# Attention bias tables: one copy of each row in DRAM, read with a stride of one number between partitions and with reversed keys

## The chip, the cores and the metric

The kernel runs on one core of one Trainium2 chip. The metric is the device time of one execution in microseconds (us). The engines are TensorE (PE, matrix products), VectorE (DVE), ScalarE (ACT), GpSimd (POOL) and SyncE (SP), which here only issues transfers.

## What is computed

The reference chains two networks on 256 tokens of width 1024, in float32. The first is one layer: a gated feed-forward network (`ffn1`), attention, a second feed-forward network (`ffn2`) and a per-layer embedding. The second is two layers with a latent attention, a long convolution and a feed-forward network, with modulation vectors (`w_mod`). The change touches only the attention of the first layer. It has 16 heads in two mixers, both with a causal window and an additive bias that depends on the head and on the distance of query and key alone:

```python
rel = jnp.arange(bq)[:, None] + max_dist - jnp.arange(nk)[None, :]
bias = rel_bias[t5_bucket(rel * stride)].astype(jnp.float32)
...
logits = jnp.where(valid[None, :, None, None], logits + bias, NEG_INF)
```

## The kernel before

Every product of two float32 matrices is made of three products of split operands (a rounded part and a rest, `hi` and `lo`): `gemm` (L126 to L128) and `gemm_T` (L139 to L141). Weights come in tiles `raw` of 512 KB, two k tiles each, which SP loads (L111, in `units`). ACT rounds each k tile to `whi` (L115) and DVE takes the rest, `wlo` (L116). There are 4 buffers for `raw` and 16 each for `whi` and `wlo`, so that loading runs ahead of PE by that much and no more.

`ffn1` goes over 11 chunks of its inner width, in three groups (0 to 3, 4 to 7, 8 to 10). For a chunk, `up_T` makes gate and up products (`ffn1g`, `ffn1u`; 4 times 24 products of 256 columns, in two halves), ACT applies Silu (L280), DVE multiplies (L283), ACT and DVE split the result (L190, L191) into `ffn1ah` and `ffn1al`. Behind a group, `down` multiplies its chunks with `ffn_w_down` (`ffn1dn`, products of 512 columns, L126 to L128) and adds up in four PSUM banks, for two token tiles by two halves. Six banks are there for all of this; four hold these sums, so the products of a chunk have two, and a half of a chunk needs the bank that L283 of the half before has read.

Work of other kinds is put between as background steps (`bg`): the columns of the modulation vectors (L634 loads a `wmod` tile of 512 KB, two L648 on DVE use it), and one step that makes the bias tables (`bias_tables`, L352). It makes a row of 384 numbers for each of the 16 heads, by reversed distance, with one small product (`bt`, L362) and a mask (`bv`, L364). Then it writes each row 128 times to DRAM (`bscr`, L366, 16 x 128 x 384 numbers) and reads four tables `btab` back (L371), each for 4 heads with 256 numbers per partition. The stride of 383 numbers between partitions moves the row on by one number from a partition to the next:

```python
d = self.dram.tile([16, P, 384], F32, name="bscr")
nc.sync.dma_start(d, v.unsqueeze(1).broadcast_to((16, P, 384)))
```

`scores` (in `attention1`) adds a part of a table to the scores of a head, on DVE (L439): 128 columns for token tile 0 and 256 for token tile 1, two heads at a time, eight jobs.

The order of the instructions on each engine is fixed when the program is built: the kernel's text gives dependences, and a scheduler with a cost model for transfers and engines puts the instructions in order. On the chip each engine then goes strictly by its order, and SP too: a load that waits holds up all loads behind it. The tiles `btab`, `wmod` and `ffn1ah`/`ffn1al` share 24 work buffers (`k4`).

Of the kernel before, what the change touches and what calls it, by code (L numbers as in the profile page):

```python
# [10 lines left out]
F32 = mybir.dt.float32  # L11
# [23 lines left out]
K2 = 12  # L35
# work that waits for another engine goes behind so many microseconds of products
WAIT = dict(first=5.0, gain=5.0, mod=7.0, fx=5.0, ctx0=7.0, ctx=10.0, act=1.9, ka=4.0, soft1=7.0, pv1=1.0, k=5.0, q=7.0,
            soft=8.0, pv=5.5, calm=3.0, calmp=28.0)
# background steps for each 8 k tiles of products
RATE = dict(ffn1=0.37, att1=0.0, ffn2=0.6, hyena=0.4, gates=1.0, att=0.3, ffn=1.1)  # L40


class Net:
# [60 lines left out]
    def units(self, src, kts, n=512):  # L104
        """src: [P, kts, n] in DRAM; returns its k tiles, each split exactly in two float32r parts."""
        nc = self.nc
        us = []
        for k0 in range(0, kts, UK):
            k = min(UK, kts - k0)
            raw = self.raw.tile([P, k, n], F32, name="raw", tag="raw")  # L110
            nc.sync.dma_start(raw, src[:, k0:k0 + k, :])  # L111
            for j in range(k):
                hi = self.whl.tile([P, n], F32R, name="whi", tag="whi")
                lo = self.whl.tile([P, n], F32R, name="wlo", tag="wlo")
                nc.scalar.activation(hi, raw[:, j], AF.Copy)  # L115
                nc.vector.tensor_tensor(out=lo, in0=raw[:, j], in1=hi.bitcast(F32), op=ALU.subtract)  # L116
                us.append((hi, lo))
        return us

    def gemm(self, ps, X, t, us, n=512, first=True, last=True, k0=0):  # L120
        """ps += x^T w over the k tiles us, from k tile k0 of X, for its token tile t."""
        nc = self.nc
# [8 lines left out]
    def gemm_T(self, ps, X, us, ct, m=None, first=True, last=True, k0=0):  # L131
        """ps [128 columns of w, X.w tokens] over the k tiles us, from k tile k0 of X; m: a part of the tokens."""
        nc = self.nc
# [10 lines left out]
    def gemm_T_all(self, pss, X, us, order):  # L144
        """several column tiles, one half of the tokens after the other"""
        for i, m in enumerate(order):
            for ct, ps in enumerate(pss):
                self.gemm_T(ps, X, us, ct, m, i == 0, i == len(order) - 1)

    def spend(self, rows):  # L150
        """rows of products have been given to the tensor engine: what was put off may be due"""
        self.clock += rows / 2400.0
# [8 lines left out]
    def defer(self, f, wait, X=None, keys=(), tag=None):  # L161
        """f, which waits for other engines, goes behind wait microseconds of products, or before X's k tiles
        (k, t) in keys are read"""
        def run():
# [34 lines left out]
    def const_pair(self, name, src):  # L199
        """a constant [128, 1024] in two parts"""  # L200
        p = self.pair(self.k4, name, [P, D])
# [10 lines left out]
    def mm3(self, out, l, li, r, ri, start, stop):  # L212
        """out += l[li]^T r[ri] of two pairs"""
        mm = self.nc.tensor.matmul
        mm(out, l[0][li], r[0][ri], start=start, stop=False)
        mm(out, l[0][li], r[1][ri], start=False, stop=False)
        mm(out, l[1][li], r[0][ri], start=False, stop=stop)
# [8 lines left out]
    def rstd(self, parts, name):  # L226
        """(sum(parts) + eps)^-0.5; parts: sums of squares over D"""
        nc = self.nc
# [11 lines left out]
    def post_norm(self, h, f, grow, half, name):  # L240
        """h + half * rms(f) * g; f: two [P, 512] sources."""
        nc = self.nc
# [13 lines left out]
    def ffn(self, X, T, wgu, wdn, name, finish):  # L256
        """Calls finish(t, n, parts): the sum of the parts is half n of tile t of the result."""
        nc = self.nc
# [93 lines left out]
    def bias_tables(self):  # L352
        """M[p, h, j] = bias_h(128 + p - j), masked; by a matmul and a round trip through DRAM."""
        nc, a = self.nc, self.a
# [9 lines left out]
        nc.vector.tensor_tensor(out=v, in0=ps[:16, :384], in1=mk, op=ALU.add)  # L364
        d = self.dram.tile([16, P, 384], F32, name="bscr")
        nc.sync.dma_start(d, v.unsqueeze(1).broadcast_to((16, P, 384)))  # L366
        self.btab = []
        for g in range(4):
            b = self.k4("btab", [P, 4, 256])
            src = bass.AP(tensor=d.tensor, offset=d.offset + 127 + 4 * g * P * 384, ap=[[383, P], [P * 384, 4], [1, 256]])  # L370
            nc.sync.dma_start(b, src)  # L371
# [13 lines left out]
    def ple_e(self):  # L385
        """p @ w_ple_proj, token-major"""
        nc, a = self.nc, self.a
# [8 lines left out]
    def attention1(self, hs, norm, nxt):  # L396
# [10 lines left out]
        def proj(t, us, n, b, z):  # L407
            """token-major projection"""
            ps = self.mm("z")
# [6 lines left out]
        def proj_T(c, ct, us, dst, scale):  # L416
            """feature-major projection: column tile ct of chunk c of q, q, k"""
            ps = self.mm("z")
# [5 lines left out]
        def scores(j, qT, kT, kj, sink):  # L424
            """two heads (partition halves) of pair tile j: probabilities, token-major [P, 2, 384]:
            columns 0..127 token tile 0, 128..383 token tile 1."""
            b0 = 2 * j if sink else 8 + 2 * j
# [8 lines left out]
            for t in range(2):  # L436
                for i in range(2):
                    b = b0 + i
                    nc.vector.tensor_tensor(out=L[:, i, cs[t]], in0=ps[i][:, cs[t]],  # L439
                                            in1=self.btab[b // 4][:, b % 4, 128 * (1 - t):256], op=ALU.add)  # L440
                nc.vector.tensor_reduce(out=m[:, 2 * t:2 * t + 2], in_=L[:, :, cs[t]], axis=AX, op=ALU.max)
# [181 lines left out]
    def mod_jobs(self, layer, jobs):  # L623
        """columns of the modulation vectors; jobs: (index, streams)."""
        nc = self.nc
# [36 lines left out]
    def mod_cols(self, layer, s, i, gname):  # L662
        """(gain * (1 + scale), shift) columns; i: index of the shift."""
        nc = self.nc
# [8 lines left out]
    def gate_row(self, layer, s, i):  # L673
        """a modulation vector on the free axis of all partitions"""
        nc = self.nc
# [11 lines left out]
    def xT_mod(self, X, t, h, G, S, name, wait):  # L687
        """transposed rms(h) * G + S into tile t of X; no S: none is added"""
        nc = self.nc
# [33 lines left out]
    def sin(self, ps, b, fr):  # L723
        """sin(fr * (ps + b)) on [64, 256], the argument reduced to [-pi, pi]"""
        nc = self.nc
# [11 lines left out]
    def spectrum(self, layer):  # L737
        """spectrum of the two-sided hyena filter, in the slots of the real DFT"""
        nc, a = self.nc, self.a
# [60 lines left out]
    def hyena(self, layer, X, between):  # L800
        """The gated long convolution of all streams, feature-major in two parts."""
        nc, a = self.nc, self.a
# [3 lines left out]
        def conv(c, ct, out, us, ps=None):  # L806
            """short convolution of channel tile ct of chunk c (0: x0, 1: x1, 2: v)"""
            if ps is None:
# [117 lines left out]
    def rope(self, src, tab, t, n, out):  # L926
        """src, out: [P, n * 128], heads as (even | odd) halves"""
        nc = self.nc
# [17 lines left out]
    def begin(self, layer):  # L946
        """Returns add(s, t, h): takes tile t of residual stream s as the input of the layer."""
        S = 1 if layer else 2
# [9 lines left out]
    def layer(self, layer, old, nxt):  # L958
        """old: functions that give the tiles of the residual streams; nxt(t, h) takes the new ones."""
        nc, a = self.nc, self.a  # L960
# [309 lines left out]
class Norm:  # L1270
    """Normalized rows of a residual stream times a gain, transposed, added tile by tile."""

# [9 lines left out]
class XT:  # L1282
    """Activations with features on partitions, split in two float32r parts: k tiles of [128, w tokens]."""

# [3 lines left out]
    def part(self, k0, n, s):  # L1288
        """n k tiles of one buffer from k0, tokens s, to be written"""
        per = D // self.w  # L1290
# [4 lines left out]
    def at(self, kk, s):  # L1295
        """tokens s of a k tile, to be written"""
        per = D // self.w
# [15 lines left out]
def pack_cols(v):  # L1313
    """rows of [n * 128] vectors as [128, n] columns"""
    parts, j = [], 0
# [8 lines left out]
def kmajor(w, n0=512):  # L1324
    """[K, N] -> [N/n0, P, K/P, n0]"""
    k, n = w.shape
# [9 lines left out]
def bias_consts():  # L1336
    """by reversed distance 255 - i: one-hot T5 buckets, and the masks of both mixers"""
    d = 255 - np.arange(384)
    n = np.maximum(d, 0)
# [143 lines left out]
```

## Time and profile before

| what | value |
|---|---|
| median of 3 runs | 1810.99 us (1807.46 to 1812.31) |
| span of the profiled execution | 1805.6 us; its own time is not listed apart from the runs, whose median is 5.4 us above it |
| PE busy | 1744.5 us, 97% |
| DVE, ACT, POOL busy | 1238.2 us (69%), 864.7 us (48%), 49.0 us (3%) |
| moved by DMA | 318.77 MB, mean 177 GB/s |

The profile lists for each engine what it did and for how long, and for each idle time which event ended it. Busy time alone does not tell what a change is worth; the waits of the engine that is busy nearly always, and what ended them, do. A wait for several things is put down to the one that came last. In the views of the DMA engines the row GB/s splits the chosen stretch in 40 equal slices.

### The profile page before, as it was taken

Reading aid. Unit: us, or ns where it says so; the run is one execution under the profiler, and the core shown is the slowest. Engines: PE = TensorE matmul, PEld = TensorE weight load, DVE = VectorE, ACT = ScalarE, POOL = GpSimd, SP = SyncE. Lnnn points to the kernel's source line nnn. Section 1 sums busy time; section 2 is a strip of 40 time slices with the busy share of each in tenths; the row PEclk is TensorE's granted clock in tenths of the full one; section 3 lists DMA queues with packets and bytes.
Section 4 is the critical chain, followed back from the end, with each engine's and each line's share of the span. In section 5 each row is a group of like instructions: output and inputs, shape, how many; then the busy total and the mean of one; then the engine's idle time right before and its main releaser. Section 6 shows DMA issues by size and latency. Waiting matters only on the chain.

```text
span 1805.6 us, 26962 instructions
## 1 busy us (share of the span) xinstructions
PE 1744.5 (97%) x9982; PEld 1512.8 (84%) x9982; DVE 1238.2 (69%) x2447; ACT 864.7 (48%) x1807; POOL 49.0 (3%) x77
## 2 busy tenths in 40 slices
PE   6999699999999999999999999999999999999998
PEld 5998587798888888888888988888778898989997
DVE  5864488886558877777766887455548857775554
ACT  6543366654558523356634433332327446655443
POOL 0000000000001000021000000000000001000000
PEclk9999799999999999999999999999999999999999
DMA  8757863485545527432345657465244453555563
GB/s 281 261 189 172 235 203 117 167 275 178 161 158 179 199 71 251 164 111 90 137 158 170 226 210 261 143 209 199 69 142 139 158 191 124 167 201 191 190 199 119
DMA packets 98276, 318.77 MB, mean 177 GB/s; under 512 B 10942, under 2 KB 20576, under 8 KB 98144
## 3 DMA queue, kind: packets, MB, share of 16 engines
q1 hardware_dynamic: 96208, 312.82, 52.5%
q10 hardware_dynamic: 1936, 4.23, 0.7%
q8 instruction: 78, 1.28, 0.3%
q14 instruction: 54, 0.44, 0.1%
HBM read 301.25 MB, written 15.75 MB: 176 GB/s over the span
## 4 chain that ended last, share of the span: by engine, by line
PE 82%; DMA 8%; DVE 6%; ACT 2%; issue 1%; POOL 1%; SPq 0%; POOLq 0%; ACTq 0%; DVEq 0%
PE f2u L139 3%; PE f2u L141 3%; PE f2u L140 3%; PE f2dn L126 3%; PE f2g L139 3%; PE f2g L141 3%; PE f2g L140 3%; PE f2dn L128 3%; PE f2dn L127 3%; DMA raw<-in_ffn_w_down_dram 2%; DVE wlo L116 2%; PE O L1102 2%; PE oa L139 1%; PE oa L140 1%; PE oa L141 1%
## 5 line engine op out<-in xcount | busy, mean ns | idle before, releaser
L116 DVE TENSOR_TENSOR wlo<-raw,whi 128x512 fp32r<-128x512 f32 x844 | 546.7, 683 | 182.2 <-ACT whi L115 149.4
L115 ACT ACTIVATE whi<-raw 128x512 fp32r<-128x512 f32 x844 | 494.4, 624 | 192.8 <-PE f2dn L128 41.8
L648 DVE SCALAR_TENSOR_TENSOR wmod<-wmod,crow 128x1024 f32<-128x1024 f32 x96 | 116.2, 1219 | 0.8 <-DMA wmod<-in_w_modT_dram 0.5
L126 PE MATMUL f2dn<-whi,f2ah 128*128 128x512 f32 x264 | 103.7, 393 | 0.0
L139 PE MATMUL f2u<-fxh,whi 128*128 128x512 f32 (+1 forms) x304 | 103.2, 340 | 0.0
L139 PE MATMUL f2g<-fxh,whi 128*128 128x512 f32 (+1 forms) x304 | 103.2, 340 | 0.0
L141 PE MATMUL f2g<-fxh,wlo 128*128 128x512 f32 (+1 forms) x304 | 103.0, 339 | 0.0
L141 PE MATMUL f2u<-fxh,wlo 128*128 128x512 f32 (+1 forms) x304 | 103.0, 339 | 0.0
L140 PE MATMUL f2u<-fxl,whi 128*128 128x512 f32 (+1 forms) x304 | 103.0, 339 | 0.0
L140 PE MATMUL f2g<-fxl,whi 128*128 128x512 f32 (+1 forms) x304 | 103.0, 339 | 0.0
L128 PE MATMUL f2dn<-whi,f2al 128*128 128x512 f32 x264 | 102.9, 390 | 0.0
L127 PE MATMUL f2dn<-wlo,f2ah 128*128 128x512 f32 x264 | 102.7, 389 | 0.0
L648 DVE SCALAR_TENSOR_TENSOR mjunk<-wmod,crow 128x1024 bf16<-128x1024 f32 x64 | 77.5, 1219 | 22.6 <-DMA wmod<-in_w_modT_dram 18.4
L141 PE MATMUL hy<-lxh,wlo 128*128 128x256 f32 (+1 forms) x224 | 70.2, 317 | 0.1
L140 PE MATMUL hy<-lxl,whi 128*128 128x256 f32 (+1 forms) x224 | 70.2, 317 | 0.0
L139 PE MATMUL hy<-lxh,whi 128*128 128x256 f32 (+1 forms) x224 | 69.6, 317 | 0.0
L280 ACT ACTIVATE f2s<-f2g 128x512 f32<-128x512 f32 (+1 forms) x38 | 18.9, 496 | 99.6 <-PE f2g L141 99.6
L190 ACT ACTIVATE f2ah<-f2s 128x512 fp32r<-128x512 f32 (+1 forms) x40 | 21.3, 532 | 93.0 <-DVE f2s L283 93.0
L283 DVE TENSOR_TENSOR f2s<-f2u,f2s 128x512 f32<-128x512 f32 (+1 forms) x38 | 21.4, 562 | 63.8 <-PE f2u L141 63.8
L139 PEld LDWEIGHTS f2u<-fxh,whi 128*128 128x128 f32 x304 | 57.7, 190 | 7.6 <-issue 1.5
L139 PEld LDWEIGHTS f2g<-fxh,whi 128*128 128x128 f32 x304 | 57.7, 190 | 7.2 <-issue 0.9
L140 PEld LDWEIGHTS f2g<-fxl,whi 128*128 128x128 f32 x304 | 57.7, 190 | 6.3
(520 smaller groups left out, 4811.2 us busy)
## 6 DMA issues: line engine op xcount, KB each, us to landing
wmod<-in_w_modT_dram SPq DMA_DIRECT2D x96, 512.0 KB, 6.3
raw<-in_ffn_w_gu_dram SPq DMA_DIRECT2D x88, 512.0 KB, 5.6
raw<-in_w_gate_up_dram SPq DMA_DIRECT2D x88, 512.0 KB, 5.4
raw<-in_w_in_dram SPq DMA_DIRECT2D x80, 512.0 KB, 4.8
raw<-in_ffn_w_down_dram SPq DMA_DIRECT2D x44, 512.0 KB, 4.5
raw<-in_w_down_dram SPq DMA_DIRECT2D x44, 512.0 KB, 4.2
raw<-in_w_out_dram SPq DMA_DIRECT2D x24, 512.0 KB, 4.6
raw<-in_w_in_q_dram SPq DMA_DIRECT2D x16, 512.0 KB, 5.2
```

The lines of the kernel that those rows point to most:

```text
L115: nc.scalar.activation(hi, raw[:, j], AF.Copy)
L116: nc.vector.tensor_tensor(out=lo, in0=raw[:, j], in1=hi.bitcast(F32), op=ALU.subtract)
L126: nc.tensor.matmul(ps[:, :n], xh, hi, start=first and k == 0, stop=False)
L127: nc.tensor.matmul(ps[:, :n], xh, lo, start=False, stop=False)
L128: nc.tensor.matmul(ps[:, :n], xl, hi, start=False, stop=last and k == z)
L139: nc.tensor.matmul(ps[:, m], hi[:, c], xh, start=first and k == 0, stop=False)
L140: nc.tensor.matmul(ps[:, m], hi[:, c], xl, start=False, stop=False)
L141: nc.tensor.matmul(ps[:, m], lo[:, c], xh, start=False, stop=last and k == z)
L190: nc.scalar.activation(hi, ps, AF.Copy)
L283: nc.vector.tensor_tensor(out=s, in0=pu[:, :W], in1=s, op=ALU.mult)
L648: nc.vector.scalar_tensor_tensor(out=junk, in0=w, scalar=1.0, in1=self.crows[s], op0=ALU.mult, op1=ALU.mult, accum_out=self.modc[layer][s] ...
L1102: nc.tensor.matmul(po[:, :256], V[:, kt, g * P:(g + 1) * P], pT[:, k, :], start=k == 0, stop=k == nt - 1)
```

## The change

The rows go to DRAM once, 24 KB in place of 3072 KB. They are held by rising distance (`bias_consts`), and the table of a partition starts one number further on than that of the partition before. A key further to the right is nearer, so the table is now in reversed order of the keys, and L439 reads it backwards.

```diff
-        d = self.dram.tile([16, P, 384], F32, name="bscr")
-        nc.sync.dma_start(d, v.unsqueeze(1).broadcast_to((16, P, 384)))
+        d = self.dram.tile([16, 384], F32, name="bscr")
+        nc.sync.dma_start(d, v)
...
-            src = bass.AP(tensor=d.tensor, offset=d.offset + 127 + 4 * g * P * 384, ap=[[383, P], [P * 384, 4], [1, 256]])
+            src = bass.AP(tensor=d.tensor, offset=d.offset + 4 * g * 384, ap=[[1, P], [384, 4], [1, 256]])
...
-                                            in1=self.btab[b // 4][:, b % 4, 128 * (1 - t):256], op=ALU.add)
+                                            in1=self.btab[b // 4][:, b % 4, 0:128 * (1 + t)][:, ::-1], op=ALU.add)
...
-    d = 255 - np.arange(384)
+    d = np.arange(384) - 127
```

(Comments and docstrings are taken out as well, with the line numbers kept.)

Since the scheduler now counts a short write, it orders the end of `ffn1` in another way. On SP, behind the loads of the last two up chunks, these are the instructions before (single buffers with their numbers; in brackets the kinds of events that an instruction waits for):

```order
L366 DMA bscr_1828<-bv_1826 2048x1x384 [waits DMAHW0_49,DVE_49]
L111 DMA raw_2191<-in_ffn1_w_down_dram 128x1024 [waits DMAHW4_49,DVE_49]
L111 DMA raw_2201<-in_ffn1_w_down_dram 128x1024 [waits DMAHW5_49,DVE_49]
L371 DMA btab_1830<-bscr_1828 128x4x256 [waits DMAHW0_49]
L371 DMA btab_1832<-bscr_1828 128x4x256
L371 DMA btab_1834<-bscr_1828 128x4x256 [waits PE_49]
L371 DMA btab_1836<-bscr_1828 128x4x256 [waits DMAHW6_49,PE_49]
L634 DMA wmod_1977<-in_w_modT_dram 128x1024 [waits DMAHW7_49,PE_49]
L634 DMA wmod_1979<-in_w_modT_dram 128x1024 [waits PE_49]
L111 DMA raw_2211<-in_ffn1_w_down_dram 128x1024 [waits DMAHW1_49,DVE_49]
```

And these with the change:

```order
L366 DMA bscr_1828<-bv_1826 16x384 [waits DMAHW0_49,DVE_49]
L371 DMA btab_1830<-bscr_1828 128x4x256 [waits DMAHW0_49]
L371 DMA btab_1832<-bscr_1828 128x4x256
L371 DMA btab_1834<-bscr_1828 128x4x256 [waits PE_49]
L371 DMA btab_1836<-bscr_1828 128x4x256 [waits DMAHW4_49,PE_49]
L634 DMA wmod_1977<-in_w_modT_dram 128x1024 [waits DMAHW5_49,PE_49]
L634 DMA wmod_1979<-in_w_modT_dram 128x1024 [waits DMAHW6_49,PE_49]
L111 DMA raw_2191<-in_ffn1_w_down_dram 128x1024 [waits DMAHW7_49,DVE_49]
L111 DMA raw_2201<-in_ffn1_w_down_dram 128x1024 [waits DVE_49]
```

The first two weight loads of group three have moved behind the tables and two `wmod` loads. The last two tables and both `wmod` tiles wait for PE, which still reads the buffers that they go into.

On DVE, behind the mask of the bias rows, this is the order before:

```order
L364 TENSOR_TENSOR bv<-bt,mk 16x384
L116 TENSOR_TENSOR wlo<-raw,whi 128x512 x8
L283 TENSOR_TENSOR ffn1s<-ffn1u,ffn1s 128x256
L191 TENSOR_TENSOR ffn1al<-ffn1s,ffn1ah 128x256
L116 TENSOR_TENSOR wlo<-raw,whi 128x512 x4
L648 SCALAR_TENSOR_TENSOR mjunk,modc_83<-wmod,crow 128x1024
L283 TENSOR_TENSOR ffn1s<-ffn1u,ffn1s 128x256
L648 SCALAR_TENSOR_TENSOR wmod,modc_84<-wmod,crow 128x1024
L191 TENSOR_TENSOR ffn1al<-ffn1s,ffn1ah 128x256
```

And with the change:

```order
L364 TENSOR_TENSOR bv<-bt,mk 16x384
L116 TENSOR_TENSOR wlo<-raw,whi 128x512 x8
L648 SCALAR_TENSOR_TENSOR mjunk,modc_83<-wmod,crow 128x1024
L648 SCALAR_TENSOR_TENSOR wmod,modc_84<-wmod,crow 128x1024
L283 TENSOR_TENSOR ffn1s<-ffn1u,ffn1s 128x256
L191 TENSOR_TENSOR ffn1al<-ffn1s,ffn1ah 128x256
L116 TENSOR_TENSOR wlo<-raw,whi 128x512 x4
L283 TENSOR_TENSOR ffn1s<-ffn1u,ffn1s 128x256
```

The two L648 have moved ahead of the first L283 of the last but one up chunk. On PE, 18 of the 72 products of group three stood between the last two up chunks; with the change all 96 products of the last chunk come first, and the 72 follow in one run, ordered by token tile, so that 36 (27 before) stand behind the last one of token tile 0. ACT's operations of this stretch are reordered in the same sense. From the first scores on, the order of all engines is the same.

## Rows read from the trace of the kernel before

**Rows 1.** The page, busy time: us, share of the span, instructions of each engine.

```profile
PE 1744.5 (97%) x9982; PEld 1512.8 (84%) x9982; DVE 1238.2 (69%) x2447; ACT 864.7 (48%) x1807; POOL 49.0 (3%) x77
```

**Rows 2.** Waits of PE, 157 to 260 us: line, waited for, us, times, longest.

```profile
PE ffn1dn L126 <- ACT whi L115: 17.9, 1, 17.9
PE trm L185 <- DVE attnn L697: 1.2, 1, 1.2
PE ffn1dn L126 <- ACT ffn1ah L190: 1.2, 1, 1.2
```

**Rows 3.** Timeline of ACT, 150 to 235 us: start, us, instruction, idle before it.

```profile
162.26 5.35 ACT L115 ACTIVATE whi<-raw 128x512 fp32r<-128x512 f32 x8 [5.96 <-PE ffn1dn L128]
...
195.71 1.15 ACT L115 ACTIVATE whi<-raw 128x512 fp32r<-128x512 f32 x2 [22.04 <-DMA raw<-in_ffn_w_down_dram]
```

**Rows 4.** Waits of SP, 157 to 200 us.

```profile
SPq L371 <- DMA bscr<-bv: 19.0, 1, 19.0
```

**Rows 5.** Timeline of SP, 156 to 235 us: transfers issued.

```profile
158.48 0.67 SPq L366 DMA_DIRECT2D bscr<-bv  x1
164.28 10.92 SPq L111 DMA_DIRECT2D raw<-in_ffn_w_down_dram  x2
194.22 2.15 SPq L371 DMA_DIRECT2D btab<-bscr  x4
196.47 1.62 SPq L634 DMA_DIRECT2D wmod<-in_w_modT_dram  x2
```

**Rows 6.** DMA engines, 157 to 195 us: GB/s in 40 slices; an issue, with its size.

```profile
GB/s 349 341 280 274 244 142 99 95 99 97 99 99 92 97 102 92 99 100 95 95 111 94 105 99 92 100 100 91 99 100 95 99 95 94 126 121 212 298 313 211
...
bscr<-bv SPq DMA_DIRECT2D x1, 3072.0 KB
```

**Rows 7.** Windows: length, busy us (instructions) of each engine, granted clock, DMA share, GB/s.

```profile
178.40:196.40 18.00, 0.05 (x2) 0.01 (x1) 0.03 (x1) 0.69 (x2) 0.00 (x0) 0.60 0.87 142
196.40:203.60 7.20, 7.20 (x19) 5.39 (x20) 2.56 (x4) 1.88 (x4) 0.00 (x0) 0.58 1.07 373
203.60:215.10 11.50, 11.50 (x98) 11.50 (x97) 9.72 (x18) 6.51 (x15) 0.00 (x0) 1.00 0.81 295
```

**Rows 8.** Timeline of PE, 196 to 204 us.

```profile
202.63 0.39 PE L128 MATMUL ffn1dn<-whi,ffn1al 128*128 128x512 f32 x1
202.86 0.40 PE L126 MATMUL ffn1dn<-whi,ffn1ah 128*128 128x512 f32 x1
```

**Rows 9.** DMA engines, 196 to 210 us: packets in all.

```profile
DMA packets 2919, 5.20 MB, mean 372 GB/s; under 512 B 160, under 2 KB 2151, under 8 KB 2917
```

**Rows 10.** DMA engines, 1785 to 1791 us: 40 slices of 0.15 us; an issue.

```profile
GB/s 27 27 0 0 0 0 0 0 0 0 28 0 0 0 0 0 0 0 0 82 164 328 410 382 382 328 382 355 246 191 164 55 27 0 0 0 0 0 0 0
...
grow<-gscr SPq DMA_DIRECT2D x1, 512.0 KB
```

**Rows 11.** Timeline of DVE, 205 to 240 us.

```profile
206.04 1.22 DVE L648 SCALAR_TENSOR_TENSOR wmod<-wmod,crow 128x1024 f32<-128x1024 f32 x1
207.18 0.08 DVE L648 DVE_READ_ACCUMULATOR wmod<-wmod,crow 128x1 f32 x1
...
210.94 0.42 DVE L283 TENSOR_TENSOR ffn1s<-ffn1u,ffn1s 128x256 f32<-128x256 f32 x1
```

**Rows 12.** The page, DMA issues: count, size, median us to landing.

```profile
wmod<-in_w_modT_dram SPq DMA_DIRECT2D x96, 512.0 KB, 6.3
```

**Rows 13.** Groups of DVE by form, 260 to 305 us: busy us, mean ns, idle before.

```profile
L439 DVE TENSOR_TENSOR L<-S,btab 128x256 f32<-128x256 f32 x16 | 6.4, 414 | 0.0
L439 DVE TENSOR_TENSOR L<-S,btab 128x128 f32<-128x128 f32 x16 | 4.3, 284 | 1.1 <-PE S L435 1.1
```

**Rows 14.** The chain that ended last, 140 to 330 us, in order of time.

```profile
286.66 1.13 DVE L L439 x4
...
302.11 0.85 DVE L L439 x3
```

**Rows 15.** Groups of DVE by form, 600 to 1000 us.

```profile
L816 DVE SCALAR_TENSOR_TENSOR x<-hy,cols,x 128x510 f32<-128x510 f32 x5 | 3.7, 744 | 6.6 <-ACT x L813 6.6
...
L835 DVE TENSOR_TENSOR vv<-vv,x 128x512 f32<-128x512 f32 x4 | 2.7, 686 | 0.0
```

## Prediction, made before the changed kernel was run

> **What bounds the kernel now.** I read the page first. TensorE (PE) is busy for 97% of the span [rows 1], so a change can only gain where PE stands still or runs slowly. The next view is what PE waits for, over the whole span. One wait stands out: 17.9 us before the first down product of group three (`ffn1dn`), put down to ScalarE's rounding of a weight tile (`whi`), once, while the two waits that follow it in the same stretch are 1.2 us each [rows 2]. That the releaser is ACT says little: ACT itself sat idle for 22 us before that `whi`, waiting for the weight load from `ffn_w_down` [rows 3]. So the next view is SyncE's queue (SP), which issues these loads. It waited 19.0 us at L371 for the write of the bias scratch `bscr` to land [rows 4], and its timeline shows why: the write is issued at 158.48, and the table loads that read it back only at 194.22 [rows 5]. The DMA view of 157 to 195 us gives the price: 3072 KB, and after the last weight load in flight 27 us at 92 to 111 GB/s [rows 6]. The two weight loads issued at 164.28 and after it share the DMA engines with that write and land only with its end.
>
> The stretch by windows: from 178.4 to 196.4 PE does nothing. [...]
>
> **The change part by part.**
>
> The write falls from 3072 KB to 24 KB. At even the old write's 97 GB/s that is 0.25 us, plus a landing that no row of this size shows. I bound it by 0 and 5 us, and neither costs anything: issued at 158.5 it ends before 163.7, where the down products of group two release the buffers of the third and fourth table, and the `wmod` loads behind them need buffers that are released with the last product of that group, at about 166.8. (By the instruction rows ahead, these loads wait for PE.)
>
> The four table loads keep their size, 512 KB each in runs of 1 KB, and their count. They move: now they stand ahead of the first two `ffn_w_down` loads, and so do two `wmod` loads of 512 KB. From 196 to 210 us the same mix of loads ran at 372 GB/s [rows 9], so 2.1 MB of tables take 5.6 us and 1.05 MB of `wmod` 2.8 us. Issued between 162 and 168, all are in by about 172, and four weight loads (2.1 MB, 5.6 us) by about 178. Who needs them? In the new order PE does all of the last up chunk before any product of group three. That chunk's weights are already split: ACT's eight `whi` at 162.26 [rows 3] are its weights, and it takes 11.5 us (203.6 to 215.1 [rows 7]). So PE's first need is not 178.4 but 189.9, and 12 us of cover lie over the loads. The wait of 17.95 us and the 3.1 us at the low clock go: **21.05 us**. If the cover failed, each us the weights land after 189 would come back one for one.
>
> Reading the table rows from one place: before, 128 partitions read 128 different copies; now they read 6 KB per load, overlapping. The nearest row is the `grow` load, in which 128 partitions read one row of 4 KB: 512 KB at up to 410 GB/s, over in some 1.7 us [rows 10]. That is the same rate as the mix of rows 9, so I charge nothing.
>
> VectorE (DVE) is where the change adds a wait. In the new order its two L648 operations, which need the first `wmod` tile, stand ahead of the first L283 of the up chunk, which frees the PSUM bank that PE needs for the second half of that chunk, at 175.5 (178.4 less a quarter of 11.5). Queued behind them on DVE is everything else of this stretch. L648 takes 1.22 us and 0.08 us with its accumulator, L283 0.42 [rows 11]: 3.0 us in all, so `wmod` must land by 172.5. My estimate by rate is 171 to 173; issued at 167.2 and with the median landing of 6.3 us of all 96 such loads [rows 12] it is 173.5, a wait of 1.0 us. Ends 0 and 1.0; I take **0.6 us lost**, in the middle, since this tile is neither alone nor in heavy traffic.
>
> The reversed read of the table (L439) is 32 operations, 16 of 128 and 16 of 256 columns at 284 and 414 ns [rows 13], or 1.02 ns a column. No row reads backwards. Below, the cost is nothing (a gain is excluded, as the number of columns is the same). Above, two ticks a column: 0.13 and 0.26 us more, 6.2 us on DVE. Of this the chain that ended last holds only runs of four and three such operations [rows 14], 7 in all, 1.4 us; if all 16 of the last four score jobs counted, 3.1 us. The nearest row is the short convolution, which reads from an odd word: 744 ns for 510 columns against 686 for 512 aligned [rows 15], 0.12 ns a column, 0.7 us on DVE and under 0.2 us on the chain. I take **0.2 us lost**. [...]
>
> Two small waits follow the stall [rows 2]. The one for `ffn1ah`, 1.2 us, came of loads that were late after the stall (ACT had rounding of the next weights ahead of it); in the new order ACT reaches it at about 191.5 and PE wants it at 193: **1.2 us won**. The one for `attnn`, 1.2 us, had 27 products behind it as cover; now there are 36, 2 us more. But the same chain follows for token tile 1, where PE had no slack, so half may come back: **0.6 us won**.
>
> Sum: 17.95 + 3.1 + 1.2 + 0.6 - 0.6 - 0.2 = 22.05, so **22 us less**. Everything later moves with it, as the instruction order there is the same. The profiled span is 1805.6 us and becomes 1783.6; the median of the runs lies 5.4 us above that span (their own spread is 4.9), so the time becomes 1811.0 - 22.0 = **1789.0 us**.
>
> **The rivals.**
>
> (a) The table loads are slow, because 128 partitions read one small place. The price runs through `wmod` and DVE: with T us for the four loads, `wmod` lands at about 165 + T and PE waits T - 7.5. At 190 GB/s T is 11 and the wait 3.5: 1792. At 71 GB/s T is 29.5 and the gain is gone; below that the kernel is **slower**: at 60 GB/s T is 35 and the time 1817. For: the scratch write itself ran at 97 GB/s [rows 6], so a transfer with one small end can be this slow. Against: the `grow` load [rows 10], a read of just this kind. [...]
>
> (b) The backward read costs a second tick. DVE loses 6.2 us, PE 1.4 to 3.1: 1790.2 to 1791.9. For: nothing but the lack of a row. Against: the odd-word row costs only 0.12 ns a column [rows 15]. [...]
>
> (c) The change does not do all it says: with the scratch write gone, PE still waits, for `wmod` through DVE or for the weights behind tables and `wmod`. At a landing of 8 us instead of 6.3 and as much for the weights the wait is 3 to 6 us, and a wait of more than a few us costs clock too: 1792 to 1796. For: 3 MB now stand ahead of the weights on SP. Against: 12 us of cover.
>
> (d) The gain is given back later, in a stretch where loads are the limit and the stall had let them run ahead. Half of it: 1800. Against: raw weight buffers are four, so no more than four loads can run ahead.
>
> **How the numbers follow.** My forecast, 1787 to 1791, has 0.64. Case (b) 0.12, (c) with the mild end of (a) 0.12, (d) 0.06, the severe (a) 0.06, half of it near no change and half slower. A measurement of this kernel can tell some 0.3%, 5.4 us, from no change: faster 0.94, within 0.03, slower 0.03. The range: without losses and with both small waits gone it is 23.5 us, 1787.5, less 2.5 for the scatter of runs; upward it takes in (b) and (c) to 1796: 1785 to 1796.
>
> **What would show it.** SP's wait at L371 falls from 19.0 us to 1 to 4; no PE wait of over 3 us between 150 and 260 us; a granted clock of 1.00 throughout 178 to 210; the first attention scores (L439) some 22 us earlier; L439 at 284 to 300 and 414 to 445 ns. The sum is wrong if PE waits at the second half of the up chunk (DVE behind `wmod`), if table loads run under 190 GB/s, if L439 grows by 100 ns or more, or if the shift of L439 is 22 us but the end moves by less.

## The result, and the profile after

The changed kernel takes 1784.85 us (median of 4 runs, 1780.17 to 1788.61), the kernel before beside it 1809.22 us: a ratio of 0.987 (95% interval 0.9853 to 0.9887). The medians lie 24.4 us apart; the ratio stands for 23.5 us. A second measurement (a2 below) gave 0.9877 (0.9862 to 0.9892). The forecast, 1811.0 to 1789.0, is a ratio of 0.9879, inside both intervals. The range, 1785 to 1796, is a ratio of 0.9856 to 0.9917 to the same 1811.0 and holds the measured one. The median itself lies 0.15 us under the range's lower end, since the kernel before, too, came out 1.8 us under its base.

In the profile after (an execution of 1782.49 us, span 1780.7 us) the page gives PE the same work in a shorter span [rows 1]:

```profile
PE 1741.6 (98%) x9982; PEld 1511.5 (85%) x9982; DVE 1238.5 (70%) x2447; ACT 864.3 (49%) x1807; POOL 49.0 (3%) x77
```

The waits of PE from 150 to 260 us answer to [rows 2]; the columns are the waiting line, what it waited for, us in all, times and the longest:

```profile
PE ffn1u L139 <- DVE ffn1s L283: 1.4, 1, 1.4
PE trm L185 <- DVE attnn L697: 1.2, 2, 0.9
PE z L141 <- DVE wlo L116: 0.2, 1, 0.2
```

The waits for `whi` (17.9 us) and for `ffn1ah` (1.2 us) are gone. A wait of 1.4 us for DVE is new, and the one for `attnn` is still 1.2 us, now over two token tiles. SP's wait at L371 and its timeline, against [rows 4, 5]:

```profile
SPq L371 <- DMA bscr<-bv: 3.6, 1, 3.6
```

```profile
159.47 0.34 SPq L366 DMA_DIRECT2D bscr<-bv  x1
163.42 2.76 SPq L371 DMA_DIRECT2D btab<-bscr  x4
166.28 1.42 SPq L634 DMA_DIRECT2D wmod<-in_w_modT_dram  x2
167.79 14.28 SPq L111 DMA_DIRECT2D raw<-in_ffn_w_down_dram  x6
```

The tables are issued 4 us after the write in place of 35.7. The windows show the granted clock: 1.00 throughout, where [rows 7] had 0.60 and 0.58.

```profile
160.00:170.00 10.00, 10.00 (x54) 8.63 (x54) 5.37 (x8) 5.06 (x8) 0.00 (x0) 1.00 0.77 226
170.00:180.00 10.00, 8.60 (x72) 8.39 (x71) 4.01 (x8) 2.44 (x6) 0.00 (x0) 1.00 0.97 378
180.00:190.00 10.00, 10.00 (x86) 10.00 (x85) 6.78 (x13) 4.17 (x10) 0.00 (x0) 1.00 0.64 215
```

The new wait starts at the load of `wmod`, as the prediction had it. DVE's timeline shows it standing 5.74 us for that tile, and then both L648 before the L283 that PE waits for:

```profile
175.07 1.23 DVE L648 SCALAR_TENSOR_TENSOR mjunk<-wmod,crow 128x1024 bf16<-128x1024 f32 x1 [5.74 <-DMA wmod<-in_w_modT_dram]
176.22 0.08 DVE L648 DVE_READ_ACCUMULATOR mjunk<-wmod,crow 128x1 f32 x1
176.34 1.23 DVE L648 SCALAR_TENSOR_TENSOR wmod<-wmod,crow 128x1024 f32<-128x1024 f32 x1
177.49 0.08 DVE L648 DVE_READ_ACCUMULATOR wmod<-wmod,crow 128x1 f32 x1
177.49 0.42 DVE L283 TENSOR_TENSOR ffn1s<-ffn1u,ffn1s 128x256 f32<-128x256 f32 x1
```

And in PE's timeline the product behind it:

```profile
177.96 0.39 PE L139 MATMUL ffn1u<-ffn1h,whi 128*128 128x256 f32 x1 [1.41 <-DVE ffn1s L283]
```

The tile took 8.8 us to land (166.28 to 175.07; the landings of these tiles are not on record, so here and below the start of the L648 that waits for the tile stands for it). The DMA view from 163 to 171 us (slices of 0.2 us) shows where some of that went. The tables, whose transfers begin at about 164.5, reach 374 GB/s, sink to 133 to 184 from 166.2 to 167.6, and stay near 290 until 169.6; after that it is 380. The DMA row (busy share in tenths) says that the engines were mostly busy meanwhile:

```profile
DMA  0003000279999999489997789999998999999999
GB/s 0 0 0 82 0 0 0 77 220 276 323 312 374 374 343 271 133 143 184 154 138 148 154 261 318 287 277 297 246 287 261 333 302 343 358 379 379 389 379 384
```

Reading backwards costs nothing here; against [rows 13], the groups of DVE from 240 to 285 us:

```profile
L439 DVE TENSOR_TENSOR L<-S,btab 128x256 f32<-128x256 f32 x16 | 6.4, 413 | 0.0
L439 DVE TENSOR_TENSOR L<-S,btab 128x128 f32<-128x128 f32 x16 | 4.3, 284 | 1.1 <-PE S L435 1.1
```

Runs of the same kernel differ by some 8 us, so for the size of each effect I use two marks in PE's timeline that enclose the stretch: the bias product `bt` (L362), before which nothing differs in order, and the first scores `S` (L435). The kernel before, then the changed one:

```profile
157.06 0.81 PE L362 MATMUL bt<-oh,rb 32*16 32x384 f32 x2
...
261.52 0.93 PE L435 MATMUL S<-kTA,qTA 64*128 64x128 f32 x8
```

```profile
158.05 0.81 PE L362 MATMUL bt<-oh,rb 32*16 32x384 f32 x2
...
241.30 0.93 PE L435 MATMUL S<-kTA,qTA 64*128 64x128 f32 x8
```

That is 104.46 us before and 83.25 after: **21.2 us** of the gain arise between these marks.

### The profile page after: what moved, and what is told of

Read it like the earlier page. It is cut to its first block, busy times and chain, and to the rows that moved or that the text cites. A ratio compares the mean times of both kernels' runs of the same rounds, so it can differ in the third digit from the quotient of the medians.

```text
span 1780.7 us, 26970 instructions
## 1 busy us (share of the span) xinstructions
PE 1741.6 (98%) x9982; PEld 1511.5 (85%) x9982; DVE 1238.5 (70%) x2447; ACT 864.3 (49%) x1807; POOL 49.0 (3%) x77
## 4 chain that ended last, share of the span: by engine, by line
PE 83%; DMA 6%; DVE 6%; ACT 2%; issue 1%; POOL 1%; SPq 0%; POOLq 0%; ACTq 0%; DVEq 0%
PE f2u L139 3%; PE f2dn L126 3%; PE f2u L140 3%; PE f2u L141 3%; PE f2g L139 3%; PE f2g L140 3%; PE f2g L141 3%; PE f2dn L128 3%; PE f2dn L127 3%; DVE wlo L116 2%; PE O L1102 2%; PE trP L185 1%; PE oa L141 1%; PE oa L140 1%; PE oa L139 1%
## 5 line engine op out<-in xcount | busy, mean ns | idle before, releaser
L648 DVE SCALAR_TENSOR_TENSOR wmod<-wmod,crow 128x1024 f32<-128x1024 f32 x96 | 116.0, 1218 | 1.0 <-DMA wmod<-in_w_modT_dram 0.6
L648 DVE SCALAR_TENSOR_TENSOR mjunk<-wmod,crow 128x1024 bf16<-128x1024 f32 x64 | 77.5, 1218 | 22.0 <-DMA wmod<-in_w_modT_dram 18.3
L283 DVE TENSOR_TENSOR f2s<-f2u,f2s 128x512 f32<-128x512 f32 (+1 forms) x38 | 21.3, 562 | 63.4 <-PE f2u L141 63.4
L141 PEld LDWEIGHTS f2u<-fxh,wlo 128*128 128x128 f32 x304 | 57.7, 190 | 6.3
```

The lines of the kernel that those rows point to most:

```text
L141: nc.tensor.matmul(ps[:, m], lo[:, c], xh, start=False, stop=last and k == z)
L283: nc.vector.tensor_tensor(out=s, in0=pu[:, :W], in1=s, op=ALU.mult)
L648: nc.vector.scalar_tensor_tensor(out=junk, in0=w, scalar=1.0, in1=self.crows[s], op0=ALU.mult, op1=ALU.mult, accum_out=self.modc[layer][s] ...
```

## The experiments

All ratios are to the kernel before on the same chip, with 95% intervals. "bt to S" is the time between the two marks in the profiled execution; "PE waits" are those of `ffn1` from `bt` on.

| run | what it is | ratio (interval) | bt to S, us | PE waits, us |
|---|---|---|---|---|
| before | | 1 | 104.46 | 17.9 + 1.2 |
| change | | 0.987 (0.9853 to 0.9887) | 83.25 | 1.4 |
| a2 | change again | 0.9877 (0.9862 to 0.9892) | 82.13 | none |
| e1 | copy kept, rest of the change | 1.0052 (1.0036 to 1.0068) | 113.25 | 17.7 + 9.0 |
| e2 | change + unread copy, SP's queue | 1.0017 (1.0007 to 1.0027) | 105.27 | 21.9 |
| e3 | change + unread copy, ACT's queue | 1.0033 (1.0017 to 1.0048) | 109.38 | 24.1 + 1.3 |
| e4 | before, copy from 128 partitions | 0.9897 (0.9879 to 0.9915) | 81.93 | none |
| e5 | as e1, own copy for each partition | 1.0002 (0.999 to 1.0013) | 107.30 | 17.8 + 2.4 |
| e6 | change, rows 196608 bytes apart | 0.9939 (0.9926 to 0.9952) | 93.42 | 9.1 |
| e7 | change, rows 198144 bytes apart | 0.9888 (0.9869 to 0.9908) | 83.18 | 0.7 |
| e8 | change + a quarter of the unread copy | 0.986 (0.9842 to 0.9878) | 81.56 | none |
| v3 | change, `wmod` loads put off | 0.988 (0.9866 to 0.9894) | 81.57 | none |

**Is the write the cost, or the way the tables are read? (e1, e5)** In e1 the rows go out 128 times again, and all else is as in the change:

```diff
-        d = self.dram.tile([16, 384], F32, name="bscr")
-        nc.sync.dma_start(d, v)
+        d = self.dram.tile([16, P, 384], F32, name="bscr")
+        nc.sync.dma_start(d, v.unsqueeze(1).broadcast_to((16, P, 384)))
...
-            src = bass.AP(tensor=d.tensor, offset=d.offset + 4 * g * 384, ap=[[1, P], [384, 4], [1, 256]])
+            src = bass.AP(tensor=d.tensor, offset=d.offset + 4 * g * P * 384, ap=[[1, P], [P * 384, 4], [1, 256]])
```

> The rows are still written 128 times (3072 KB); reversed keys, the stride of one number and the read from one copy stay as in the change. The order of PE's work comes out as in the kernel before. Theory (the 128-fold write, for which SP waits ahead of the loads behind it, is the whole cost): SP waits 17 to 20 us at the table load, PE 17 to 18 us for the first down product of group three, ratio to the kernel before 0.999 to 1.001. Rival 1 (the gain comes from the way the tables are read, one small place with a stride of one number, or from the backward read): the wait stays but the time still falls, ratio 0.987 to 0.993. Rival 2 (the backward read costs something that the gain covers): ratio 1.001 to 1.003, as there is nothing to cover it now.

The stall came back, but the kernel became 9 us slower than before, which no theory had. Waits of PE, 150 to 260 us:

```profile
PE ffn1dn L126 <- ACT whi L115: 17.7, 1, 17.7
PE ffn1u L139 <- DVE ffn1s L283: 9.0, 1, 9.0
PE trm L185 <- DVE attnn L697: 1.2, 1, 1.2
```

The order on all engines is that of the kernel before, so the second wait can only come of how fast something ran. The DMA engines from 195 to 207 us (slices of 0.3 us) show it: the table loads, issued from 195.22 on, fall to 55 to 164 GB/s.

```profile
GB/s 287 314 341 355 328 358 287 256 229 178 85 164 150 109 99 75 82 55 79 113 137 109 365 379 341 304 174 198 232 263 311 277 212 205 256 246 242 362 317 239
```

`wmod`, behind them, landed 15.6 us after its issue; the kernel before needed 8.1, issued at 196.47 [rows 5] and used by DVE so:

```profile
204.55 1.23 DVE L648 SCALAR_TENSOR_TENSOR mjunk<-wmod,crow 128x1024 bf16<-128x1024 f32 x1 [5.56 <-DMA wmod<-in_w_modT_dram]
```

e5 takes one thing from e1: partition p reads from copy p.

```diff
-            src = bass.AP(tensor=d.tensor, offset=d.offset + 4 * g * P * 384, ap=[[1, P], [P * 384, 4], [1, 256]])
+            src = bass.AP(tensor=d.tensor, offset=d.offset + 4 * g * P * 384, ap=[[385, P], [P * 384, 4], [1, 256]])
```

> The 128-fold write kept and the keys reversed, as in the first run, but partition p reads from copy p (a stride of 385), so that no two partitions read the same place. In the first run the tables and wmod behind them landed 8 us later than before and PE waited 9 us more. Theory R (128 partitions reading one place of one copy are slow): here the first wmod tile lands 8 us after its issue again, PE's second wait is under 1 us, ratio 0.999 to 1.001. Theory S (the reversed keys or the backward read cost it): the second wait of 7 to 9 us stays, ratio 1.004 to 1.007.

It came out as theory R: 1.0002, no wait for `ffn1s`, and 297 to 464 GB/s from 198.7 us on (the same view from 196 to 208 us):

```profile
GB/s 379 219 246 205 191 164 167 188 249 389 365 386 379 386 386 375 359 304 297 365 369 359 362 358 358 362 389 352 427 399 369 423 423 396 437 396 464 369 382 382
```

So the write is the cost, the backward read and the reversed keys cost nothing that can be told, and reading one copy from all partitions can be slow.

**Why was e1 slow and the change not? (e6, e7)** Both read one place with 128 partitions; the rows lie 1536 bytes apart in the change and 196608 in e1. e6 gives the change the distance of e1; e7 adds 1536 bytes to that:

```diff
-        d = self.dram.tile([16, 384], F32, name="bscr")
-        nc.sync.dma_start(d, v)
+        d = self.dram.tile([16, P * 384], F32, name="bscr")
+        nc.sync.dma_start(d[:, :384], v)
...
-            src = bass.AP(tensor=d.tensor, offset=d.offset + 4 * g * 384, ap=[[1, P], [384, 4], [1, 256]])
+            src = bass.AP(tensor=d.tensor, offset=d.offset + 4 * g * P * 384, ap=[[1, P], [P * 384, 4], [1, 256]])
```

> The changed kernel, with its 16 rows not side by side in 24 KB but each 196608 bytes from the next, where the first run read them; one small write, as in the change. Theory R1 (reading rows that lie so far apart, each by 128 partitions, is slow by itself): the first wmod tile lands 13 to 16 us after its issue, PE waits 6 to 9 us for ffn1s, ratio 0.990 to 0.994. Theory R2 (the first run's reads were slow because they came right behind the large write to the same buffer): 8 to 9 us and 1 to 2 us as in the change, ratio 0.986 to 0.988.

```diff
-        d = self.dram.tile([16, P * 384], F32, name="bscr")
+        d = self.dram.tile([16, (P + 1) * 384], F32, name="bscr")
...
-            src = bass.AP(tensor=d.tensor, offset=d.offset + 4 * g * P * 384, ap=[[1, P], [P * 384, 4], [1, 256]])
+            src = bass.AP(tensor=d.tensor, offset=d.offset + 4 * g * (P + 1) * 384, ap=[[1, P], [(P + 1) * 384, 4], [1, 256]])
```

> As the run with rows 196608 bytes apart, but 198144 apart: 1536 bytes more, the pitch that the rows have in the change. Everything else is the same. Theory T (the distance was bad because it is three times 65536, so that the rows of a load meet in the same part of DRAM): the rate comes back, the first wmod tile lands 8 to 10 us after its issue, PE waits 0 to 2 us for ffn1s, ratio 0.986 to 0.989. Theory U (rows far apart are slow at any distance, each being one small place that 128 partitions read): the wait of 7 to 9 us and the ratio of 0.993 to 0.995 stay.

e6 came out as R1: half of the gain gone, without any large write. Its waits of PE, a window behind the first of them (granted clock 0.50, so this wait cost clock as well), and from 164 to 176 us its DMA engines and the issue of the tables (count, size, us to landing, which is on record for the last of the four alone):

```profile
PE ffn1u L139 <- DVE ffn1s L283: 9.1, 1, 9.1
PE trm L185 <- DVE attnn L697: 1.2, 2, 0.9
```

```profile
185.20:188.00 2.80, 1.67 (x8) 1.67 (x9) 1.63 (x5) 1.46 (x4) 0.00 (x0) 0.50 0.44 180
```

```profile
GB/s 0 0 0 65 55 79 106 147 72 147 65 44 174 72 44 147 58 99 137 61 181 294 358 273 246 225 208 201 270 324 341 304 311 273 307 297 297 283 331 355
...
btab<-bscr SPq DMA_DIRECT2D x4, 512.0 KB, 14.0
```

e7 came out as T. The same view, 166 to 178 us:

```profile
GB/s 0 55 0 10 140 283 239 263 208 167 178 130 184 345 355 355 345 369 358 311 290 188 174 181 283 324 386 382 427 423 430 423 423 423 423 437 341 437 396 423
...
btab<-bscr SPq DMA_DIRECT2D x4, 512.0 KB, 7.4
```

The last table lands in 7.4 us in place of 14.0, and PE's wait is 0.7 us. With all partitions reading one place, the distance between the rows decided here, not that it is large: 0.8% more than 196608 bytes brought the rate back. The distance is not enough by itself: the kernel before and e5 have the same 196608 bytes, but each partition reads a copy of its own, and `wmod` landed there 8.1 and 7.9 us after its issue. Why 196608 bytes were slow, no run shows; the cause that theory T names was its assumption.

**What about the write costs? (e2, e3)** Both keep the change and add a write of 3072 KB that nothing reads, on SP's queue or on ScalarE's:

```diff
-            nc.sync.dma_start(b, src)
-            self.btab.append(b)
+            nc.sync.dma_start(b, src); self.btab.append(b)
+        nc.sync.dma_start(self.dram.tile([16, P, 384], F32, name="bdum"), v.unsqueeze(1).broadcast_to((16, P, 384)))
```

> The changed kernel with the old 3072 KB write added behind the small one, on SP's queue, to a scratch that nothing reads, so that no instruction waits for it. Theory A (what costs is that SP's instruction waits for the write to land): SP's wait stays at 4 us and the time is that of the change, ratio 0.987 to 0.989. Theory B (what costs is the write itself, ahead of the loads in the same queue: about 31 us at the 99 GB/s that the kernel before shows): the tables and the first wmod tile land only at about 192, the wait moves from SP's instruction to VectorE's L648 and through it to PE, some 17 us with the low clock behind it, ratio 0.998 to 1.002. Theory C (the loads share the DMA engines with it and go on at a part of their rate): a PE wait of 3 to 8 us, ratio 0.990 to 0.995.

In e3 the last line reads `nc.scalar.dma_start`.

> As the run before, but the unread 3072 KB write is issued on ScalarE's queue. Theory B (the write holds up what stands behind it in its own queue): nothing of this stretch stands behind it on ScalarE's queue, so the loads on SP go on, PE waits 1 to 3 us, ratio 0.987 to 0.990. Theory C (the write holds up everything, as all queues share the same 16 DMA engines): as on SP's queue, PE waits 10 us or more, ratio 0.994 to 1.002. If it is the sharing at part rate, both runs come out alike, near 0.990 to 0.995.

e2 came out near theory B: SP waited 3.3 us for the small write, was then held 29.6 us at issuing the four table loads, and PE stood 21.9 us; the ratio is 1.0017. So no wait for the large write is needed. But e3 shows that theory B is not the whole cause: nothing of this stretch stands behind the write in ScalarE's queue, and PE waited 24.1 us (a ratio of 1.0033, a little above what any theory had). The size of this wait can't be held against e2's, as the scheduler put L648 further ahead on DVE in e3. Theory C holds in its harder form: the write takes up the DMA engines that SP's loads need too. In e3 the queue rows of the DMA view, 160 to 190 us, show it (q10 is ScalarE's queue, q1 SP's; packets, MB, share of the time of 16 engines):

```profile
q10 hardware_dynamic: 1939, 2.98, 85.1%
q1 hardware_dynamic: 956, 1.14, 10.3%
```

For 2.98 MB the write holds 85.1% of the engines' time, so at full occupation it would run, as an estimate, at 2.98 MB / (0.851 x 30 us) = 117 GB/s; the loads get 10.3%, and in that share of the time they move 369 GB/s. These means hide two phases. From 164 to 175 us the write's queue alone moved anything, though SP had begun to issue the tables at 162.00; from 176 to 190 SP's queue moved 0.84 MB, 60 GB/s, beside the write. Why the first phase is there the runs don't show. The queue rows of 164 to 175 us, and then of 176 to 190:

```profile
q10 hardware_dynamic: 702, 1.08, 89.4%
```

```profile
q10 hardware_dynamic: 863, 1.33, 84.7%
q1 hardware_dynamic: 838, 0.84, 16.7%
```

Behind the write in its own queue it is harder still. In the kernel before, from 163 to 188 us, the queue moved 1580 packets, all of under 2 KB. These are the write's 1536 bytes; a packet of the weight loads has 4096 (from 120 to 126 us, with weight loads, the 360 packets of over 2 KB make up the queue's 1.47 MB), and none came through, though the first was issued at 164.28:

```profile
DMA packets 1581, 2.44 MB, mean 98 GB/s; under 512 B 0, under 2 KB 1580, under 8 KB 1580
```

**Why is the write so slow? (e4)** The kernel before with its rows computed on 128 partitions, each eight times (the mask is loaded eight times over as well), so that every partition writes 16 of the copies:

```diff
-        nc.tensor.matmul(ps[:16, :384], rb, oh, start=True, stop=True)
+        nc.vector.tensor_copy(out=rb8.rearrange("p (h c) -> p h c", h=16), in_=rb.unsqueeze(2).broadcast_to((32, 16, 8)))
+        nc.tensor.matmul(ps[:, :384], rb8, oh, start=True, stop=True)
...
-        nc.sync.dma_start(d, v.unsqueeze(1).broadcast_to((16, P, 384)))
+        nc.sync.dma_start(d.rearrange("h (c j) n -> (h c) j n", c=8), v.unsqueeze(1).broadcast_to((P, 16, 384)))
```

> The kernel before (128-fold copy, forward read with the stride of 383), but its rows are computed on 128 partitions, each row eight times, and every partition writes 16 of the 128 copies: the same 3072 KB into the same scratch, from 128 partitions in place of 16. Theory P (16 source partitions limit the write to the 97 GB/s of the trace): from 128 partitions it runs at 250 GB/s or more, lands within 13 us, SP's wait falls to 5 to 10 us, PE's stall to under 2 us, ratio 0.987 to 0.991: then the change's gain could have been had with the copy kept. Theory Q (the limit lies in DRAM or in descriptors of 1.5 KB): the write stays at about 100 GB/s, SP waits 17 to 20 us, ratio 0.998 to 1.002.

Theory P holds. The DMA engines now run at 350 to 440 GB/s (163 to 174 us), against 97 in [rows 6], and SP's wait is 5.0 us. Some weight packets are among them: from 170 to 174 us, 940 of 965 packets have the size of the write's (948 less 8), an estimate of 360 GB/s for the write alone:

```profile
GB/s 372 313 164 89 149 223 240 356 393 423 393 356 397 391 402 402 402 391 402 391 413 380 385 380 397 439 380 363 380 380 385 402 402 369 385 374 352 371 350 404
```

```profile
DMA packets 965, 1.51 MB, mean 378 GB/s; under 512 B 8, under 2 KB 948, under 8 KB 965
```

```profile
SPq L371 <- DMA bscr<-bv: 5.0, 1, 5.0
```

Between the marks it gains 22.5 us, as much as the change, with the whole copy kept; its ratio, 0.9897, isn't told apart from a2's. SP's order is that of the kernel before; on PE 16 products of group three, not 18, stand between the last two up chunks, and a new order alone is not what gains, as e2 and e3 have the change's order on PE and lose all of it. The number of source partitions set the rate: 97 GB/s from 16, an estimated 360 from 128. Why a write from 16 is slow, no run shows.

**How much cover is there, and can the last wait go? (e8, v3, a2)** e8 is e2 with 32 copies (768 KB) in place of 128.

> The changed kernel with an unread write on SP's queue behind the small one, as in the second run, but a quarter as large (768 KB, 32 copies). By the rate of 97 to 99 GB/s it takes 7.9 us of all DMA engines. If the cover over the wmod tile is as good as used up in the change (its wait was 0 to 1.4 us there), nearly all of that comes back: PE waits 7 to 10 us for ffn1s, with the low clock behind it some 9 to 12 us of time, ratio 0.992 to 0.995. If there is a cover of 8 us or more, as the prediction had it for the weights (12 us), the time is that of the change: 0.986 to 0.989.

The first of the two cases failed: there was no wait, and the ratio is 0.986. That is the number of the second case, but not for its reason. The write took its time (98 GB/s) and `wmod` was in only at 179.18. But in this build the scheduler put one more L283 ahead of L648 on DVE; PE needed the next one only then:

```profile
174.17 0.42 DVE L283 TENSOR_TENSOR ffn1s<-ffn1u,ffn1s 128x256 f32<-128x256 f32 x1 [4.46 <-PE ffn1u L141]
179.18 1.23 DVE L648 SCALAR_TENSOR_TENSOR mjunk<-wmod,crow 128x1024 bf16<-128x1024 f32 x1 [3.67 <-DMA wmod<-in_w_modT_dram]
180.33 0.42 DVE L283 TENSOR_TENSOR ffn1s<-ffn1u,ffn1s 128x256 f32<-128x256 f32 x1
```

So the cover hangs on DVE's order, which an added transfer changes, and e8 didn't measure the cover of the changed kernel itself. e2 has e8's order, and its 21.9 us are with that larger cover. v3 makes the four table loads a background step of their own, so that `wmod` comes later on SP and L648 later on DVE:

```diff
-        nc.sync.dma_start(d, v)
-        self.btab = []
+        nc.sync.dma_start(d, v); self.btab = []; self.bscr = d
+    def bias_load(self, nc, d):
...
-        self.bg = self.mod_jobs(0, [(0, both)]) + [("bias", self.bias_tables)] + self.mod_jobs(0, [(1, both)])
+        self.bg = self.mod_jobs(0, [(0, both)]) + [("bias", self.bias_tables), ("bias", lambda: self.bias_load(self.nc, self.bscr))] + self.mod_jobs(0, [(1, both)])
```

> The changed kernel with its four table loads as a background step of their own, so that the two wmod loads that stood right behind them on SP come later, behind the weights, and VectorE's L648 with them. If the wait of 1.4 us for ffn1s comes of wmod behind the tables: it is gone, and the ratio is that of the change or 0.001 less. If the later background steps come too late for their users, a new wait of 1 us or more stands in the later stages and the ratio is 0.001 to 0.004 above that of the change.

> The changed kernel as it is, on the chip of the three runs below, so that they can be held against it: ratio to the kernel before 0.985 to 0.989, PE's wait for ffn1s 1 to 2 us, the first wmod tile 8 to 9 us from issue to landing.

In v3 the wait is gone and the stretch is 1.7 us shorter than in the change's first profile, 0.6 than in a2's; its ratio, 0.988, is the same as the change's. In a2 the wait expected at 1 to 2 us wasn't there at all: `wmod` landed 7.5 us after its issue in place of 8.8. The wait lies within the scatter of a landing, and no version tried here beats the change by what can be measured.

## Why the prediction was right

- **The stall, 17.95 us, and the low clock, 3.1 us: right in cause and size.** With the copy kept (e1, e5) the stall is there; with the copy kept but fast (e4) it is gone, though the text of the kernel has nothing else of the change. The 3.1 us are an estimate from [rows 7, 8]: the 7.2 us at 0.58, less the 18 products of 128x512 in them (196.39 to 203.55 us in PE's timeline) at 0.23 us each. In that stall the granted clock was 1.00 up to 181.5 us, 3.1 us into it, and 0.50 from 182 on; behind the change's wait of 1.4 us it was 1.00. The clock's part was not measured by itself: of the 21.2 us between the marks the lists of waits make 17.5, which leaves 3.7 for it and for gaps too short to be listed. The prediction said that the weight loads share the DMA engines with the write. In the kernel before they did not even do that; behind the write in SP's queue they moved nothing until it was nearly over. From another queue (e3) loads were starved as well (10.3% of the engines' time), so SP's wait is not needed. The prediction did not ask why 97 GB/s was the write's rate, and so didn't see that the copy could stay.
- **`ffn1ah`, 1.2 us: right**; the wait is gone.
- **`attnn`, 0.6 us won: wrong.** It is 1.2 us still, for two token tiles: it came back in full, where the prediction had half. The step that failed is the cover. Of the 36 products behind the last one of token tile 0, 12 stand behind the transposes (`trm`) that wait, so 24 cover them, and not 36; before, all 27 did. PE's `ffn1dn` products up to those transposes and behind them:

```profile
192.40:207.10 14.70, 13.79 (x60) 11.13 (x60) 1.38 (x2) 1.96 (x6) 1.00 0.42 125
207.10:210.70 3.60, 2.76 (x12) 2.18 (x12) 0.23 (x1) 0.09 (x1) 1.00 0.81 279
```

- **`wmod` through DVE to L283, 0.6 us lost: right in place, mis-sized.** It was 1.41 us in one profile and nothing in the other. The median landing of 6.3 us [rows 12] was the wrong row: behind four table loads it was 8.1 us in the kernel before, 8.8 and 7.5 after. The tile was issued at 166.28, ahead of the forecast 167.2, which took back a part.
- **The table loads at no charge: not right.** The `grow` load [rows 10] was taken as the nearest row; it reads one row of 4 KB, the tables many overlapping pieces of 1 KB. Their rate sank to 133 to 184 GB/s from 166.2 to 167.6 us. Rival (a) was real, with the pitch of the rows as its condition (196608 bytes slow, 198144 not), which the prediction did not have; e6 is what it had priced. At 19.3 us from the first table's issue to `wmod` in use, PE lost 9.1 us.
- **The backward read, 0.2 us lost: nothing** (413 and 284 ns against 414 and 284).

Sum to the first scores: 22.25 us forecast (the backward read comes later), 21.2 measured in one profile and 22.3 in a2. The prediction's other base, 5.4 us from the profiled span to the median, held 1.8 us around the span (1782.49 against 1780.7 after) and some 3.6 of scatter. Given back later (rival (d)) was nothing that can be seen: the whole gain, 24.4 and 21.8 us in the two measurements, lies about that of the stretch, within the scatter. The absolute miss of 4.2 us is 1.8 in the base (1811.0 against 1809.2) and 2.4 in the gain, whose interval is 20.4 to 26.6; so the 22.0 us are right within the noise, but the losses and gains of under 1 us in the sum are too small for the time to bear out.

## What to carry to other kernels

A transfer that nobody reads can still stop TensorE (21.9 us in e2, 24.1 in e3): ask what share of the DMA engines it holds for how long (85.1% of 30 us in e3), and put no bulky write with few source partitions ahead of weights, in their own queue or in another. A transfer's rate hung on its shape on both sides: spread a write over all partitions (97 GB/s from 16, an estimated 360 from 128), and mind the pitch of rows that many partitions read at once (192 KB was bad here, a last table landing after 14.0 us; 1.5 KB more was good, 7.4 us). And when a stall goes, price the next load in line from a landing behind the same queue of transfers, not from the median of all.

## What was not expected of the hardware

- The same 3072 KB to the same DRAM buffer: 97 GB/s from 16 partitions, an estimated 360 from 128, with the DMA engines nearly full in both (SP's queue held 88.9% of their time from 163 to 188 us in the kernel before, 100.9% from 163 to 174 in e4).
- Loads beside the slow write: none of their packets for 25 us behind it in its own queue, none for 11 us and then 60 GB/s from another queue.
- Rows 196608 bytes apart, each read by 128 partitions one number apart: 44 to 174 GB/s for the first 5 us; 198144 apart, 130 to 370.
- An operand read backwards on DVE: 413 ns for 256 columns, 414 forwards.
